# Grouped-query attention of the second mixer: probabilities divided before the value product, values held by TensorE on halves of its columns, result with channels on partitions

## The chip, the cores and the metric

The kernel runs on one core of one Trainium2 chip. The metric is device microseconds (us) of one execution. The kernel before takes 1529.04 us, the median of three runs (1528.59 to 1533.04).

## The reference, cut to what matters

The network is one step of a diffusion model on 256 latent tokens and 256 context tokens of width 1024, with two layers. The first layer has one kind of mixer and a dense feed-forward part; the second has the mixer of this case and a mixture of eight experts. In the second layer only the latent tokens are still needed behind the mixer.

```python
def odd_mixer(h, hc, ...):                         # second layer, need_ctx is False
    q, k, v, gate, xr = split(h @ w_in)            # 8 query heads, 2 key/value heads, 64 each
    qc, kc, vc, gatec, xrc = split(hc @ w_in)
    q = axial_rope(rms_norm(q, qn_g)); k = axial_rope(rms_norm(k, kn_g)); kc = rms_norm(kc, kn_g)
    k_all, v_all = concat([kc, k]), concat([vc, v])        # 512 keys
    s = einsum('bqngd,bknd->bngqk', q, k_all) * 64 ** -0.5
    p = softmax(s, axis=-1)                                # n: 2 key/value heads, g: 4 query heads of each
    y_attn = einsum('bngqk,bknd->bqngd', p, v_all)         # 256 tokens x 512 channels (n, g, d)
    a, bterm = lru_coeffs(conv(xr), ...)                   # for both directions
    y_rec = (linear_scan(forward) + linear_scan(backward)) * gelu(gate)   # 256 x 512
    return concat([y_attn, y_rec])

x = x + g1 * (y @ w_out[1])                        # output projection, 1024 x 1024
x = x + g2 * moe_swiglu(rms_norm(x) * (1 + sc2) + sh2)     # router, top 2 of 8 experts
```

## The kernel before

**Staging.** The program goes through the first layer, then the second mixer, its output projection, the router and the experts. Weights come from HBM through the SyncE queue into a ring of buffers; each dense weight is split on arrival into a rounded part `whi` (ACT, L215) and a remainder `wlo` (DVE L217, during the projection a quarter of it on POOL L219), and a dense product is three TensorE products (L233 to L235). The expert weights are not split; their loads need the numbers of the experts that are used, which the router writes, so they wait in the SyncE queue for DVE's `slot` (L1348).

**What sets the order.** Each engine runs its instructions in the order in which the program writes them. Side work is written as generators: `spawn` starts one, `pump` between the products of a running projection lets each one advance, and `yield n` means that it goes on at the n-th pump from there. So `yield 3` leaves three pumps' worth of other work, on every engine, between what stands ahead of it and what stands behind it. Beside the mixer's own projections (`xr`, then `gate`) these generators run: the recurrence's coefficients and its scans (`lru`, DVE L1049, L1056, L1057, with squares on POOL L1034 and the final sums on POOL L1063, L1064), and the attention.

**The attention.** `attention` starts one `attend1` for each of two query blocks `b` of 128 tokens and four groups `g`, two pumps apart. One of them handles the two heads (n = 0, 1) that share `g`:

- the score product `sp` (128 queries on partitions, 512 keys), one for each head, on 64 rows of TensorE (L1073);
- the softmax: maximum on DVE (L693), exponential on ACT with the sum of its row accumulated into one column of `S` (L694). `P` is not divided;
- `yield 3`, then four 128x128 transposes of `P` for each head into `pt` (L1082), and a copy `PT` to SBUF, by ACT for n = 0 (L1087), by DVE for n = 1 (L1085);
- `yield 1`, then four products for each head (L1093): TensorE holds `PT` (128 keys by 128 queries) and `v` moves, 64 columns, into 64 columns of `po`. `po` has the queries on partitions.

Behind g = 3 come one reciprocal of the eight sums (L1095) and one product of `po` with it into `yr[b]` (L1097): the division of the softmax. There is one `po` for each query block.

**The output projection.** `out_proj` (L643) needs `y` with channels on partitions, in eight tiles of 128 channels, as a rounded part `y1h` and a remainder `y1l`. Tiles 4 to 7 are the recurrence's and already lie so; they are multiplied first. Tiles 0 to 3 are the attention's: `y_tile` transposes two 128x128 blocks of `yr[0]` and `yr[1]` (L1871) and splits the result out of PSUM (L635, L636). A tile is made two tiles ahead of its use. This is done once, for the first 512 output columns; the second 512 use the same tiles. `w_out` of this layer comes as four loads of 512x512 (two halves `h` of the rows, two of the columns), the rows of a load as four blocks of 128 on partitions (`plan_out`, L638).

After the projection come the norm, the router, the gathering of tokens and the experts, which store the result.

## Time and profile before

| What | Value |
|---|---|
| Median of three runs | 1529.04 us (1528.59 to 1533.04) |
| The profiled execution, its own time | 1531.24 us |
| Its span | 1529.4 us |
| TensorE clock granted, mean | 0.984 of full speed |
| PE matmul busy | 1453.7 us, 95% |
| PE weight load busy (overlaps PE) | 866.3 us, 57% |
| DVE busy | 682.0 us, 45% |
| ACT busy | 356.2 us, 23% |
| POOL busy | 145.3 us, 9% |
| Moved by DMA | 400.94 MB, mean 262 GB/s |

The engines' names are those of the profile: PE is TensorE, DVE VectorE, ACT ScalarE, POOL GpSimd, SP SyncE. A row of work gives its start, its duration, the line and tile, shapes as partitions x elements and, in brackets, idle time of the engine ahead of it and what ended it. The averages over the span hide the stages: PE is busy 95% of it, and the share says little of what sets the time in a given stage. The span and the profiled execution's own time differ by 1.8 us, which lies around the span.

### The profile page before, as it was taken

Reading aid. Unit: us, or ns where it says so; the run is one execution under the profiler, and the core shown is the slowest. Engines: PE = TensorE matmul, PEld = TensorE weight load, DVE = VectorE, ACT = ScalarE, POOL = GpSimd, SP = SyncE. Lnnn points to the kernel's source line nnn. Section 1 sums busy time; section 2 is a strip of 40 time slices with the busy share of each in tenths; the row PEclk is TensorE's granted clock in tenths of the full one; section 3 lists DMA queues with packets and bytes.
Section 4 is the critical chain, followed back from the end, with each engine's and each line's share of the span. In section 5 each row is a group of like instructions: output and inputs, shape, how many; then the busy total and the mean of one; then the engine's idle time right before and its main releaser. Section 6 shows DMA issues by size and latency. Waiting matters only on the chain.

```text
span 1529.4 us, 24172 instructions
## 1 busy us (share of the span) xinstructions
PE 1453.7 (95%) x10208; PEld 866.3 (57%) x10208; DVE 682.0 (45%) x1131; ACT 356.2 (23%) x576; POOL 145.3 (9%) x154
## 2 busy tenths in 40 slices
PE   5999899999999999988987999999999999999996
PEld 3766667878788887866666433343433333345442
DVE  3646875787878886387875401010010100011133
ACT  3425442422222222253753100100000000000000
POOL 1230212000000005033224000000000000000000
PEclk9999999999999999999998899999999999999999
DMA  9433454254556684132045899999999999999996
GB/s 349 151 113 108 151 186 145 83 184 146 165 193 199 222 273 132 56 99 82 29 126 217 303 417 417 417 398 369 418 417 418 417 387 418 415 413 415 376 414 250
DMA packets 151798, 400.94 MB, mean 262 GB/s; under 512 B 10185, under 2 KB 38217, under 8 KB 151681
## 3 DMA queue, kind: packets, MB, share of 16 engines
q1 hardware_dynamic: 150688, 396.69, 68.5%
q8 instruction: 82, 1.34, 0.3%
q10 hardware_dynamic: 576, 1.57, 0.3%
q0 software_dynamic: 416, 1.05, 0.3%
q14 instruction: 36, 0.29, 0.1%
HBM read 397.14 MB, written 2.15 MB: 261 GB/s over the span
## 4 chain that ended last, share of the span: by engine, by line
PE 78%; DVE 10%; POOL 4%; ACT 4%; DMA 2%; issue 2%; SPq 0%; DVEq 0%; ACTq 0%; POOLq 0%
PE ph L1548 25%; PE py L1548 12%; PE ph L235 5%; PE ph L234 5%; PE ph L233 5%; PE py L235 3%; PE py L234 2%; PE ps L233 2%; PE ps L234 2%; PE ps L235 2%; PE py L233 2%; PE ph L1552 1%; DVE wlo L217 1%; POOL hrs L240 1%; PE ptg L1596 1%
## 5 line engine op out<-in xcount | busy, mean ns | idle before, releaser
L1548 PE MATMUL ph<-raw,xt 128*32 128x512 f32 (+1 forms) x3840 | 402.1, 558 | 1.1 <-DMA raw<-in_moe_w_dram 1.1
L1548 PEld LDWEIGHTS ph<-raw,xt 128*32 128x32 f32 x3840 | 142.7, 110 | 234.1 <-issue 225.9
L1548 PE MATMUL py<-raw,gt 128*32 128x512 f32 x1760 | 195.6, 592 | 0.0
L215 ACT ACTIVATE whi<-raw 128x2048 fp32r<-128x2048 f32 x58 | 111.1, 1915 | 195.4 <-issue 61.6
L217 DVE TENSOR_TENSOR wlo<-raw,whi 128x2048 fp32r<-128x2048 f32 (+1 forms) x58 | 133.1, 2295 | 47.6 <-ACT whi L215 47.3
L1582 DVE TENSOR_TENSOR silu<-silu,ph 128x512 f32<-128x512 f32 (+3 forms) x33 | 20.6, 623 | 299.8 <-PE ph L1548 266.1
L235 PE MATMUL ph<-hTh,wlo 128*128 128x512 f32 (+1 forms) x384 | 146.2, 381 | 0.8 <-DVE wlo L217 0.8
L234 PE MATMUL ph<-hTl,whi 128*128 128x512 f32 (+1 forms) x384 | 145.3, 378 | 0.0
L233 PE MATMUL ph<-hTh,whi 128*128 128x512 f32 (+1 forms) x384 | 144.6, 377 | 0.0
L1548 PEld LDWEIGHTS py<-raw,gt 128*32 128x32 f32 x1760 | 70.9, 110 | 118.1 <-issue 108.4
L440 DVE SCALAR_TENSOR_TENSOR macc<-raw,cv,macc 128x512 f32<-128x512 f32 x154 | 111.1, 750 | 2.4 <-DMA raw<-in_w_mod_dram 1.2
L233 PE MATMUL ps<-whi,hTh 128*128 128x512 f32 (+1 forms) x272 | 108.4, 404 | 4.0 <-ACT hTh L165 2.1
L234 PE MATMUL ps<-wlo,hTh 128*128 128x512 f32 (+1 forms) x272 | 105.2, 390 | 0.0
L235 PE MATMUL ps<-whi,hTl 128*128 128x512 f32 (+1 forms) x272 | 104.9, 389 | 0.0
L1602 ACT ACTIVATE gt<-ptg 128x512 f32<-128x512 f32 (+3 forms) x18 | 9.5, 529 | 313.6 <-PE ptg L1596 313.6
L234 PEld LDWEIGHTS ph<-hTl,whi 128*128 128x128 f32 x384 | 72.7, 189 | 15.3
L233 PEld LDWEIGHTS ph<-hTh,whi 128*128 128x128 f32 x384 | 73.0, 190 | 14.6
L235 PEld LDWEIGHTS ph<-hTh,wlo 128*128 128x128 f32 x384 | 72.8, 190 | 14.9 <-DVE wlo L217 1.0
L1704 DVE TENSOR_TENSOR yacc<-yacc,py 128x512 f32<-128x512 f32 (+1 forms) x13 | 8.6, 667 | 143.4 <-PE py L1548 110.8
L234 PE MATMUL py<-wlo,gh 128*128 128x512 f32 x176 | 69.1, 393 | 0.4 <-DVE wlo L217 0.4
L233 PE MATMUL py<-whi,gh 128*128 128x512 f32 x176 | 67.8, 391 | 0.0
L235 PE MATMUL py<-whi,gl 128*128 128x512 f32 x176 | 66.9, 395 | 0.0
(362 smaller groups left out, 1748.6 us busy)
## 6 DMA issues: line engine op xcount, KB each, us to landing
raw<-in_moe_w_dram SPq DMA_DIRECT2D x216, 1024.0 KB, 12.7
raw<-in_w_mod_dram SPq DMA_DIRECT2D x48, 1024.0 KB, 5.2
raw<-in_moe_w_dram SPq DMA_DIRECT2D x64, 768.0 KB, 14.9
raw<-in_ffn_w_dram SPq DMA_DIRECT2D x33, 1024.0 KB, 5.3
raw<-in_e_w_in_dram SPq DMA_DIRECT2D x10, 1024.0 KB, 6.9
raw<-in_w_out_dram SPq DMA_DIRECT2D x8, 1024.0 KB, 6.4
raw<-in_o_w_in_dram SPq DMA_DIRECT2D x7, 1024.0 KB, 5.4
ga<-dram SPq DMA_DIRECT2D x6, 512.0 KB, 5.1
```

The lines of the kernel that those rows point to most:

```text
L215: nc.scalar.activation(hi, raw, AF.Copy)
L217: nc.vector.tensor_tensor(lo[:, :, n:], raw[:, :, n:], hi[:, :, n:], op=ALU.subtract)
L233: mm(o, lh, rh, start=start, stop=False)
L234: mm(o, lh, rl, start=False, stop=False)
L235: mm(o, ll, rh, start=False, stop=stop)
L240: g.tensor_tensor(out, out, self.mhalf[:, 0:out.shape[-1]] if len(out.shape) == 2 else self.mhalf, op=ALU.pow)
L440: v.scalar_tensor_tensor(a, raw[:, k], c, a, op0=ALU.mult, op1=ALU.add)
L1548: mm(out[ss, 0:n], lhs[:, ss], w[r][:, cs], start=first, stop=last, tile_position=(0, s * 32))
L1552: mm(out[s * 32:s * 32 + 32, 0:256], lhs, w[:, s * 256:(s + 1) * 256], start=first, stop=last, tile_position=(0, s * 32))
L1582: v.tensor_tensor(s, s, o, op=ALU.mult)
L1596: nc.tensor.transpose(pt[:, f * m:(f + 1) * m], st[t][q][h][0:m, f * 128:(f + 1) * 128], self.ident[0:m, 0:m])
L1602: nc.scalar.activation(dst, src, AF.Copy)
```

## The change

Four things are changed together.

1. The division moves ahead of the transposes. Each step has its own `S` of two columns; right behind the two exponentials DVE takes the reciprocal, and `P` is multiplied by it, on POOL for n = 0 and on DVE for n = 1. The step then waits four pumps instead of three.
2. The value product is turned. TensorE holds `v` (128 keys by 64 channels) on half of its columns, n = 0 on the first, n = 1 on the second, and `PT` moves, 128 queries. The two heads' products alternate. `po` has channels on partitions (n, d), and 128 columns for each `g`. Behind g = 3, `yr[b]` is a copy of `po`.
3. `y_tile` makes tiles 0 to 3 without transposes: two splits out of `yr[0]` and `yr[1]`, each half as wide.
4. The channels of tile g are now (n, d) for one g and not 128 neighbours of (n, g, d), so the rows of `w_out` that meet them are loaded in that order: two loads of 64 partitions in place of one of 128, for both column halves of h = 0.

```diff
--- before.py
+++ after.py
@@ -639,7 +639,12 @@
         for c in range(2):
             for h in halves:
                 src = self.I["w_out"][l, h * 512:(h + 1) * 512, c * 512:(c + 1) * 512]
-                self.plan_w(("out", l, c, h), src.rearrange("(k p) f -> p k f", p=128), (4, 512))
+                if l == 1 and h == 0:
+
+                    parts = [(n * 64, n * 64 + 64, src[n * 256:(n + 1) * 256].rearrange("(k p) f -> p k f", p=64)) for n in range(2)]
+                else:
+                    parts = src.rearrange("(k p) f -> p k f", p=128)
+                self.plan_w(("out", l, c, h), parts, (4, 512))
 
     def out_proj(self, l, y_tile, yT, blocks, halves, gates, done):
 
@@ -1063,18 +1068,22 @@
             nc.gpsimd.tensor_tensor(h[0], h[0], h[1], op=ALU.add)
             nc.gpsimd.tensor_tensor(yr[2 + t // 2][:, (t % 2) * 256:(t % 2 + 1) * 256], h[0], gate[:, t], op=ALU.mult)
 
-    def attend1(self, b, g, po, S, qT, kT, v, yr):
+    def attend1(self, b, g, po, qT, kT, v, yr):
 
         nc = self.nc
         Ps = []
+        S = self.mp.tile([128, 2], F32, tag="ssum8", name="ssum8", bufs=4)
         for n in range(2):
             ns = slice(n * 64, (n + 1) * 64)
             sp = self.ps("sp")
             nc.tensor.matmul(sp, qT[ns, g, b * 128:(b + 1) * 128], kT[ns], start=True, stop=True)
             P = self.row("P")
-            self.softmax(sp, 512, P, S[:, n * 4 + g:n * 4 + g + 1])
+            self.softmax(sp, 512, P, S[:, n:n + 1])
             Ps.append(P)
-        yield 3
+        nc.vector.reciprocal(S, S)
+        for n, P in enumerate(Ps):
+            (nc.vector if n else nc.gpsimd).tensor_scalar(P, P, S[:, n:n + 1], None, op0=ALU.mult)
+        yield 4
         PTs = []
         for n in range(2):
             pt = self.ps("pt")
@@ -1087,14 +1096,13 @@
                 nc.scalar.activation(PT, pt, AF.Copy)
             PTs.append(PT)
         yield 1
-        for n in range(2):
-            h = (n * 4 + g) * 64
-            for kb in range(4):
-                nc.tensor.matmul(po[:, h:h + 64], PTs[n][:, kb * 128:(kb + 1) * 128], v[:, kb, n * 64:(n + 1) * 64], start=kb == 0, stop=kb == 3)
+        for kb in range(4):
+            for n in range(2):
+                ns = slice(n * 64, (n + 1) * 64)
+                nc.tensor.matmul(po[ns, g * 128:(g + 1) * 128], v[:, kb, ns], PTs[n][:, kb * 128:(kb + 1) * 128], start=kb == 0, stop=kb == 3,
+                                 tile_position=(0, n * 64))
         if g == 3:
-            nc.vector.reciprocal(S, S)
-            v3 = lambda a: a.rearrange("p (h d) -> p h d", d=64)
-            nc.vector.tensor_tensor(v3(yr[b]), v3(po), S.unsqueeze(2).broadcast_to([128, 8, 64]), op=ALU.mult)
+            nc.vector.tensor_copy(yr[b], po)
 
     def plan_in1(self):
         w = self.I["o_w_in"][0]
@@ -1176,9 +1184,8 @@
                     yield 1
                 for b in range(2):
                     po = self.ps("po")
-                    S = self.mp.tile([128, 8], F32, tag="ssum8", name="ssum8", bufs=2)
                     for g in range(4):
-                        self.spawn(self.attend1(b, g, po, S, qT, kT, v, yr))
+                        self.spawn(self.attend1(b, g, po, qT, kT, v, yr))
                         yield 2
 
             def conv(t, ps):
@@ -1866,10 +1873,9 @@
 
                     def y_tile(t):
                         if t < 4:
-                            pt = self.ps()[:, 0:256]
                             for b in range(2):
-                                nc.tensor.transpose(pt[:, b * 128:(b + 1) * 128], yr[b][:, t * 128:(t + 1) * 128], self.ident)
-                            self.split_evac(yT[0][:, t], yT[1][:, t], pt)
+                                bs = slice(b * 128, (b + 1) * 128)
+                                self.split(yT[0][:, t, bs], yT[1][:, t, bs], yr[b][:, t * 128:(t + 1) * 128])
                         else:
                             self.split(yT[0][:, t], yT[1][:, t], yr[t // 2][:, (t % 2) * 256:(t % 2 + 1) * 256])
 
```

In the following listings a name with a number is one particular buffer; line numbers of the changed kernel are higher by 5 to 9 (L1056, L1057 become L1061, L1062; L1073 L1079; L1082 L1091; the copy of `pt` into `PT` L1085 becomes L1094; L1093 becomes L1102; L1034 L1039; L1063, L1064 become L1068, L1069). In the changed kernel L1085 is the scaling of `P`.

DVE at the end of the attention, before: the last two copies of `PT`, the scans of the recurrence (L1056, L1057), the reciprocal and the product that ends the attention.

```order
L1085 COPY PT<-pt 128x512
L1057 SCALAR_TENSOR_TENSOR iv_5083<-X,hc,iv_5083 128x256
L1056 SCALAR_TENSOR_TENSOR hc<-xd,iv_5082 128x256
L1049 TENSOR_TENSOR iv_5083<-iv_5083,R 128x512
L1057 SCALAR_TENSOR_TENSOR iv_5082<-xd,hc,iv_5082 128x256
L1056 SCALAR_TENSOR_TENSOR hc<-X,iv_5083 128x256
L1085 COPY PT<-pt 128x512
L1057 SCALAR_TENSOR_TENSOR iv_5083<-X,hc,iv_5083 128x256
L1095 RECIPROCAL ssum_5802<-ssum_5802 128x8
L1097 TENSOR_TENSOR yr<-po,ssum_5802 128x512
```

The same place afterwards, from the copy of `PT` of the last but two step on.

```order
L1094 COPY PT<-pt 128x512
L1083 RECIPROCAL ssum_6027<-ssum_6027 128x2
L1061 SCALAR_TENSOR_TENSOR hc<-X,iv_5083 128x256
L1085 TENSOR_SCALAR P<-P,ssum_6027 128x512
L1062 SCALAR_TENSOR_TENSOR iv_5083<-X,hc,iv_5083 128x256
L1061 SCALAR_TENSOR_TENSOR hc<-xd,iv_5082 128x256
L1094 COPY PT<-pt 128x512
L1062 SCALAR_TENSOR_TENSOR iv_5082<-xd,hc,iv_5082 128x256
L1061 SCALAR_TENSOR_TENSOR hc<-X,iv_5083 128x256
L1062 SCALAR_TENSOR_TENSOR iv_5083<-X,hc,iv_5083 128x256
L1094 COPY PT<-pt 128x512
L1105 COPY yr<-po 128x512
```

The division's two instructions stand between the scans; the scan that stood between the last copy and the attention's end stands ahead of the last copy, and the old reciprocal is gone.

PE at the same place, before: scores `sp`, transposes `pt`, value products `po` of the last three steps, then the first product of the output projection (L233).

```order
L1073 MATMUL sp<-kT_5051,qT_5050 128x512 x2
L1093 MATMUL po<-v_5052,PT 128x64 x8
L1082 MATMUL pt<-cst,P 128x128 x8
L1073 MATMUL sp<-kT_5051,qT_5050 128x512 x2
L1093 MATMUL po<-v_5052,PT 128x64 x8
L1082 MATMUL pt<-cst,P 128x128 x16
L1093 MATMUL po<-v_5052,PT 128x64 x16
L233 MATMUL ps<-whi,y1h 128x512
```

And afterwards.

```order
L1079 MATMUL sp<-kT_5051,qT_5050 128x512 x2
L1091 MATMUL pt<-cst,P 128x128 x8
L1102 MATMUL po<-PT,v_5052 64x128
L1079 MATMUL sp<-kT_5051,qT_5050 128x512 x2
L1091 MATMUL pt<-cst,P 128x128 x2
L1102 MATMUL po<-PT,v_5052 64x128 x7
L1091 MATMUL pt<-cst,P 128x128 x14
L1102 MATMUL po<-PT,v_5052 64x128 x16
L1091 MATMUL pt<-cst,P 128x128 x8
L1102 MATMUL po<-PT,v_5052 64x128 x8
L233 MATMUL ps<-whi,y1h 128x512
```

Each step's `po` now stands ahead of the last transposes of the step behind it, and the last 8 transposes stand behind 16 `po` products of earlier steps; before, 16 transposes stood in a row ahead of the last 16 `po` products.

POOL in the second half of the attention and beside the projection's start, before: squares of the recurrence (L1034), its sums (L1063, L1064) and a quarter of a weight's remainder (L219).

```order
L1034 TENSOR_TENSOR a_5761<-xd 128x512
L1063 TENSOR_TENSOR iv_5082<-iv_5082,iv_5083 128x256
L1034 TENSOR_TENSOR a_5798<-X 128x512
L1063 TENSOR_TENSOR iv_5082<-iv_5082,iv_5083 128x256
L1064 TENSOR_TENSOR yr<-iv_5082,gate_5053 128x256 x2
L1034 TENSOR_TENSOR a_5933<-xd 128x512
L219 TENSOR_TENSOR wlo<-raw,whi 128x4x128
L1034 TENSOR_TENSOR a_5978<-X 128x512
L1063 TENSOR_TENSOR iv_5082<-iv_5082,iv_5083 128x256
L1064 TENSOR_TENSOR yr<-iv_5082,gate_5053 128x256
L1063 TENSOR_TENSOR iv_5082<-iv_5082,iv_5083 128x256
L1064 TENSOR_TENSOR yr<-iv_5082,gate_5053 128x256
```

And afterwards, from the sixth scaling on.

```order
L1068 TENSOR_TENSOR iv_5082<-iv_5082,iv_5083 128x256
L1085 TENSOR_SCALAR P<-P,ssum_5889 128x512
L1039 TENSOR_TENSOR a_5946<-xd 128x512
L1069 TENSOR_TENSOR yr<-iv_5082,gate_5053 128x256 x2
L219 TENSOR_TENSOR wlo<-raw,whi 128x4x128
L1039 TENSOR_TENSOR a_5990<-X 128x512
L1085 TENSOR_SCALAR P<-P,ssum_5972 128x512
L1085 TENSOR_SCALAR P<-P,ssum_6027 128x512
L1068 TENSOR_TENSOR iv_5082<-iv_5082,iv_5083 128x256
L1069 TENSOR_TENSOR yr<-iv_5082,gate_5053 128x256
L1068 TENSOR_TENSOR iv_5082<-iv_5082,iv_5083 128x256
L1069 TENSOR_TENSOR yr<-iv_5082,gate_5053 128x256
```

The scalings stand among the recurrence's instructions, the last two of them ahead of the sums of its last two tiles.

On SP's queue the two loads of `w_out` with h = 0 are two of `64x4x512` in place of one of `128x4x512`; all else stands in the same order, except that one of the two halves of the last of them is issued ahead of the loads of the norm's and router's constants and not behind them.

## Rows read from the trace of the kernel before

**Rows 1.** Busy time by stages, columns as the first line names them
```profile
core 0: us, PE busy (x) PEld busy (x) DVE busy (x) ACT busy (x) POOL busy (x), PEclk, DMA share, GB/s
...
745.00:777.00 32.00, 31.24 (x206) 23.88 (x205) 28.86 (x43) 27.36 (x50) 7.28 (x8) 1.00 0.20 67
777.00:794.00 17.00, 11.44 (x82) 9.56 (x82) 15.30 (x23) 9.73 (x19) 6.27 (x5) 0.94 0.32 108
794.00:812.00 18.00, 17.77 (x74) 13.72 (x74) 9.47 (x20) 6.76 (x11) 6.21 (x5) 0.87 0.91 315
...
900.00:1500.00 600.00, 598.93 (x5792) 231.29 (x5788) 58.27 (x90) 37.73 (x67) 0.00 (x0) 1.00 1.01 408
```

**Rows 2.** SyncE's queue: issue of expert loads (start, us); its wait (us, times, longest)
```profile
847.04 50.68 SPq L208 DMA_DIRECT2D raw<-in_moe_w_dram  x22
...
SPq L1478 <- DVE slot L1348: 15.4, 1, 15.4
```

**Rows 3.** PE in order of time: start, us, line, tile, count, idle before
```profile
751.99 2.00 PE L1093 MATMUL po<-v,PT 128*128 128x64 f32 x16
753.79 0.36 PE L233 MATMUL ps<-hTh,whi 128*128 128x256 f32 x1
...
792.53 1.97 PE L1093 MATMUL po<-v,PT 128*128 128x64 f32 x8 [2.61 <-DVE PT L1085]
```

**Rows 4.** DVE in order of time, columns as in rows 3
```profile
736.08 0.69 DVE L1027 SCALAR_TENSOR_TENSOR iv<-iv,xd 128x512 f32<-128x512 f32 x1 [2.94 <-ACT iv L1024]
...
756.37 0.17 DVE L1095 RECIPROCAL ssum<-ssum 128x8 f32<-128x8 f32 x1
756.47 1.10 DVE L632 SCALAR_TENSOR_TENSOR gate<-gelu,gate 128x256 f32<-128x256 f32 x1
...
758.68 1.52 DVE L1056 TENSOR_TENSOR_SCAN hc<-xd,iv 128x256 f32<-128x256 f32 x1
...
770.36 0.69 DVE L1027 SCALAR_TENSOR_TENSOR iv<-iv,xd 128x512 f32<-128x512 f32 x1 [1.56 <-ACT iv L1024]
...
791.24 0.66 DVE L1056 TENSOR_TENSOR_SCAN hc<-X,iv 128x256 f32<-128x256 f32 x1
791.82 0.66 DVE L1085 COPY PT<-pt 128x512 f32<-128x512 f32 x1
...
794.54 0.69 DVE L1097 TENSOR_TENSOR yr<-po,ssum 128x512 f32<-128x512 f32 x1 [1.31 <-PE po L1093]
```

**Rows 5.** DVE by line and shape: count, busy us, mean ns, idle before
```profile
L713 DVE TENSOR_SCALAR P<-P,ssum,nlam 128x512 f32<-128x512 f32 x8 | 4.4, 545 | 0.3
```

**Rows 6.** POOL: one instruction in time, and one line by shape
```profile
758.12 1.54 POOL L1034 TENSOR_TENSOR a<-X 128x512 f32<-128x512 f32 x1
...
L1760 POOL COPY G2q<-ga 32x256 f32<-32x256 f32 x4 | 1.6, 393 | 0.1
```

**Rows 7.** PE column groups and whole array; then the chain that ended last
```profile
162.20 1.92 PE L388 MATMUL pmod<-raw,cv 128*32 128x512 f32 x16
...
762.08 1.88 PE L1023 MATMUL plru<-xd,bd 128*128 128x512 f32 x4
...
937.71 1.86 PE ph L1548 x16
...
945.04 20.74 PE ph L1548 x192
```

**Rows 8.** PE in the output projection, in order of time
```profile
799.55 0.38 PE L1871 MATMUL ps<-cst,yr 128*128 128x128 f32 x2
...
800.00 0.40 PE L234 MATMUL ps<-wlo,y1h 128*128 128x512 f32 x1
800.24 0.39 PE L235 MATMUL ps<-whi,y1l 128*128 128x512 f32 x1
```

**Rows 9.** SyncE's queue: issue of the last `w_out` load
```profile
799.15 0.71 SPq L208 DMA_DIRECT2D raw<-in_w_out_dram  x1
```

**Rows 10.** DMA issues by line: count, KB each, median us to landing
```profile
raw<-in_w_out_dram SPq DMA_DIRECT2D x8, 1024.0 KB, 6.4
```

## The prediction

> **What bounds the kernel now.** I read the stages first, then the queue that feeds the end, then the chain of waits backwards from there, and last the one engine that the chain names.
>
> The stages [rows 1] split the program behind 730 us into three. From 900 us to the end the DMA share is 1.01 at 408 GB/s: the experts' weights stream without a break, so this part takes the time that its bytes take. What can move is when it starts. The SyncE queue [rows 2] shows that: 22 expert loads go out together at 847.04, and the wait ahead of them (15.4 us) is for DVE's `slot`, the result of the router. Whatever brings the router later by a microsecond brings the end later by one.
>
> Ahead of the router stands the output projection, ahead of that the attention. The projection's first product runs behind the last `po` product on PE, and that one sat 2.61 us idle for DVE's copy of `PT` [rows 3]. That copy starts at 791.82 [rows 4]. DVE is busy 28.86 us of the 32 from 745 to 777, and 15.30 of the 17 from 777 to 794 [rows 1]; most of its own rest in the second is the 1.31 us ahead of `yr`, behind the copy [rows 4]. PE is as full until 777 (31.24 of 32) but has 5.6 us to spare after it. So in the stretch that ends the attention DVE's queue is the bound, PE second; a microsecond of DVE work put ahead of that copy counts, a microsecond taken from PE there mostly doesn't.
>
> **The change part by part.** All differences are to the median of 1529.04. The profiled run took 1531.24 (span 1529.4), 2.2 above the median; the sum is a difference made inside that execution and is put on the median.
>
> *DVE work added.* Each of the eight (query block, group) steps gets a reciprocal of two sums and a scaling of one 128x512 tile. A reciprocal starts at 756.37 and the next instruction at 756.47: 0.10 us. The same scaling in the first layer lasts 0.545 [rows 5]; neighbours overlap a little (a scan of 0.66 us at 791.24 is followed at 791.82 [rows 4]), so I count 0.50. Eight times 0.60 is 4.8. One old reciprocal goes from ahead of the last copy (0.1). By the order, the last step of the recurrence (a scan, 0.66), which stood behind the last copy, now stands ahead of it. Sum 5.4 us.
>
> *What is free of it.* The first two steps fall where DVE idles 2.94 us in one place (ahead of 736.08 [rows 4]): 1.2 us off, 4.2 left. From 745 to 777 DVE idles 3.14 us [rows 1], 1.56 of it in one wait for ACT [rows 4]. The new work fills such holes only if it isn't itself waiting: at the second block's second group the reciprocal stands directly behind its two maxima, so DVE, with everything behind it, waits there for two exponentials on ACT. Bounds 0 and 3.14; I take 1.5 as filled, since half the idle is that one wait and a new wait stands beside it. 2.7 left. `yr` is a copy now and not a product with the sums: same place, same size (0.69), nothing.
>
> *POOL.* It gets eight scalings of 128x512; no row shows this operation there. Below it is a copy of 32x256 at 0.39 us, above it a two-operand product of 128x512 at 1.54 [rows 6]. I take 0.8, as there is one operand, but twice the columns of the copy. POOL itself is free (7.28 of 32 us), and what is queued behind a scaling that waits for DVE's reciprocal are squares and sums of the recurrence and, at the end, the sums that make `yr` of the second half, needed 4 us into the projection. POOL's work is not free for DVE though: while POOL ran the product at 758.12, DVE's scan took 1.52 instead of 0.66, and the one before 1.10 [rows 4, 6]. That is 0.86 lost in 1.54, 0.55 per microsecond of POOL, for instructions with both operands in SBUF; maxima and copies out of PSUM are about half of what runs here, and I put no loss on them. Six scalings of 0.8 at half of 0.55 are 1.3 us; bounds 0 and 6 x 1.54 x 0.55 = 5.1. Sum 4.0.
>
> *PE.* A `po` block of 16 takes 1.80 us now (751.99 to 753.79 [rows 3]). Afterwards two heads share the columns. Upper bound: no overlap, 1.80. Lower: full overlap, 0.90. The nearest row is the modulation's products on four column groups, 16 of 512 columns in 1.92 us, where the whole array takes 1.88 for 4 of them [rows 7]; so they do overlap, and I take 1.0. On DVE's schedule that gain reaches the end only in the last block, and there it is undone: by the order the transposes of the last group stand behind the third group's `po`, which waits for its own copy, so after DVE's last but one copy PE still has 16 products, 8 transposes, one more DVE copy and the last block. Net 0, bounds -1.0 and +1.5.
>
> The Trainium skill (TensorEngine Tiling (Array Packing), Key Properties) says that a change of the tiling mode drains TensorE, which speaks against the halves. The trace agrees as to size: 16 expert products right after transposes take 1.86 us, in an unbroken run of 192 they take 20.74 / 12 = 1.73 [rows 7], 0.13 per return. Two switches in each of eight blocks would be 2 us of PE, inside the bounds above.
>
> *Output projection.* Eight transposes go, in four pairs. A pair starts at 799.55 and the second product behind it at 800.00; one product without it takes 0.24 [rows 8]: a pair costs 0.21, four 0.84. PE is dense there (17.77 us of the 18 from 794 to 812 [rows 1]), so this counts: -0.84. The evacuations from PSUM become splits from SBUF, eight of half the width on ACT and DVE instead of four; they stand behind `yr` with four tiles of products until the first is used: hidden, and if the cover were gone, half a microsecond for the first pair.
>
> *DMA.* Two loads of `w_out` become two halves each. The first is asked for two tiles ahead of its use. The second half of the other is issued where the whole one is now, at 799.15 [rows 9], for the projection's second half of columns, which PE, dense until 812, reaches some 10 us later. A whole one lands in 6.4 us [rows 10], so both are covered; if a half took double, the second would be 3 us late. One half moves ahead of the loads of `BA` in SyncE's queue; its buffer is released by DVE and ACT no later than theirs, so I put nothing on it.
>
> Sum: 5.4 - 1.2 - 1.5 + 1.3 + 0 - 0.84 = +3.2 us, 1532.2. With the bounds: 4.2 - 3.14 + 0 - 1.0 - 0.84 = -0.8 (1528.3) and 4.2 + 5.1 + 1.5 - 0.84 = +10 (1539).
>
> **Rivals.**
> 1. *PE was the bound.* Then eight blocks fall from 1.80 to 1.0 and the pairs go: -6.4 - 0.84, some 1522. For it: PE's 31.24 of 32 us until 777. Against it: PE's long wait at the end is for DVE [rows 3], and DVE's work grows.
> 2. *The two scalings shut each other out.* Both start on the same reciprocal, one on POOL, one on DVE. If the scaling on DVE, and every two-operand instruction beside POOL's, stands still for as long as POOL runs, six times 0.8 to 1.54 is 4.8 to 9.2 instead of 1.3: +6.7 to +11, 1535.7 to 1540; middle 1538. It decides from 0.25 us more per pair than I counted. For it: the row of 1.52; against it: only about half the instructions there can be hit. The Trainium skill (SBUF — State Buffer, Who interferes with whom) states it as a rule: VectorE in a two-port mode, which such a scaling may use, and GpSimd exclude each other for a whole instruction. The slowed scan agrees with exclusion; no row of before has a VectorE scaling beside GpSimd.
> 3. *It changes nothing at the end*, because what DVE gains in work fits in its idle time (3.14 and the 2.94) and the removed pairs pay for the rest: 1529 to 1530.
>
> **How the numbers follow.** Forecast 0.55, rival 1 0.12, rival 2 0.25, rival 3 0.08. The forecast's own range is 1528.3 to 1536. A difference of 0.3% (4.6 us; 1524.4 to 1533.6) is what a measurement can tell from none. Of the forecast's 0.55 I put 0.12 above 1533.6. Faster 0.12; within 0.43 + 0.08 = 0.51; slower 0.12 + 0.25 = 0.37. The range goes from 1526 (part of the way to rival 1) to 1538 (middle of rival 2).
>
> **What would show it.** The first projection product should start at about 798 instead of 794.3, still behind a DVE copy of `PT`, and the expert loads at about 850. DVE's scalings near 0.5 us and POOL's near 0.8 confirm the sizes; scalings of 1 us or more on DVE are rival 2. A `po` block near 1.0 us confirms the halves; if the attention then ends before 790, rival 1 holds. Wrong altogether I am if the span behind 847 changes length, or if a wait for `w_out` appears.

## The result, and the profile after

The changed kernel takes 1548.03 us (median of four runs, 1545.11 to 1551.15), the kernel before 1531.01 us (four runs, 1528.59 to 1533.04). The ratio is 1.0112, with a 95% interval from 1.0097 to 1.0127: slower by 17 us. I had forecast 1532.2 us, 3.2 more than before, with a range to 1538. The profiled execution took 1546.02 us (span 1544.2), 14.8 more than the one of before.

The stages of the changed kernel, to be held against [rows 1]:

```profile
core 0: us, PE busy (x) PEld busy (x) DVE busy (x) ACT busy (x) POOL busy (x), PEclk, DMA share, GB/s
745.00:777.00 32.00, 25.82 (x142) 15.77 (x142) 27.42 (x41) 20.22 (x37) 9.63 (x7) 0.84 0.21 66
777.00:794.00 17.00, 12.57 (x98) 9.04 (x96) 14.89 (x24) 14.99 (x26) 11.26 (x7) 1.00 0.28 93
794.00:812.00 18.00, 13.53 (x81) 10.45 (x82) 13.35 (x31) 5.45 (x18) 5.43 (x5) 0.81 0.47 125
900.00:1500.00 600.00, 597.47 (x5730) 234.99 (x5726) 56.57 (x87) 36.84 (x65) 0.00 (x0) 1.00 1.02 404
```

From 745 to 777 us PE is busy 25.8 of 32 us where it had 31.2, at a mean granted clock of 0.84 where it had 1.00. DVE is no busier. And the stage that I took for fixed, 900 to 1500, moves 404 GB/s instead of 408.

SyncE's queue, the issue of the 272 expert loads that wait for `slot` (eight more go out ahead of it; start, then time from first to last issue), of before and of the changed kernel:

```profile
847.04 651.90 SPq L208 DMA_DIRECT2D raw<-in_moe_w_dram  x272
```

```profile
857.29 658.52 SPq L208 DMA_DIRECT2D raw<-in_moe_w_dram  x272
```

The first load goes out 10.25 us later, and the 272 of them take 6.6 us longer. So there are two losses. The program in five pieces, read in the same way in every run; the marks are the first score product (`sp`), the first projection product, the first and the last expert load:

| us | before | changed | difference |
|---|---|---|---|
| start to first `sp` | 726.95 | 727.55 | +0.6 |
| `sp` to projection | 67.3 | 77.9 | +10.6 |
| projection to first load | 52.8 | 51.8 | -1.0 |
| first to last load | 651.9 | 658.5 | +6.6 |
| last load to end | 30.5 | 28.4 | -2.1 |

The first piece ends between 724.35 and 729.91 in the runs below, also where no edit touches its work, and why is open; so I compare the pieces, and call the second and third together the way from `sp` to the loads: 120.1 us before, 129.7 now.

Where the 10.6 us go shows on PE in order of time (columns as in [rows 3]):

```profile
745.41 0.28 PE L234 MATMUL ps<-hTl,whi 128*128 128x256 f32 x1
745.53 0.28 PE L235 MATMUL ps<-hTh,wlo 128*128 128x256 f32 x1
749.20 0.69 PE L1102 MATMUL po<-PT,v 128*64 128x128 f32 x2 [3.39 <-ACT PT L1096]
749.82 2.08 PE L1028 MATMUL plru<-xd,bd 128*128 128x512 f32 x2
751.82 1.97 PE L1102 MATMUL po<-PT,v 128*64 128x128 f32 x14
753.72 2.01 PE L1028 MATMUL plru<-xd,bd 128*128 128x512 f32 x2
...
759.59 1.09 PE L1102 MATMUL po<-PT,v 128*64 128x128 f32 x16 [0.35 <-ACT PT L1096]
...
765.67 1.02 PE L1028 MATMUL plru<-xd,bd 128*128 128x512 f32 x2
769.13 0.66 PE L1102 MATMUL po<-PT,v 128*64 128x128 f32 x2 [2.44 <-ACT PT L1096]
769.73 2.07 PE L1028 MATMUL plru<-xd,bd 128*128 128x512 f32 x2
771.73 1.50 PE L1102 MATMUL po<-PT,v 128*64 128x128 f32 x14
...
804.46 1.09 PE L1102 MATMUL po<-PT,v 128*64 128x128 f32 x14 [0.31 <-DVE PT L1094]
805.48 0.51 PE L233 MATMUL ps<-whi,y1h 128*128 128x512 f32 x1
```

PE ends a product at 745.8 and waits 3.39 us for ACT's copy `PT`. Behind the wait it is slow: 14 `po` products take 1.97 us where 16 take 1.09 at 759.59, and two `plru` products 2.0 where four take 1.9 before [rows 7]. The same happens, smaller, at 769. The granted clock falls there, shown with the same stretches of before below it:

```profile
core 0: us, PE busy (x) PEld busy (x) DVE busy (x) ACT busy (x) POOL busy (x), PEclk, DMA share, GB/s
...
745.60:749.20 3.60, 0.21 (x3) 0.00 (x1) 3.60 (x4) 3.57 (x8) 0.00 (x0) 0.93 0.22 16
749.20:755.70 6.50, 6.50 (x22) 2.90 (x22) 5.78 (x11) 3.30 (x5) 1.56 (x1) 0.51 0.40 153
755.70:768.00 12.30, 10.64 (x79) 7.78 (x78) 11.14 (x17) 7.76 (x15) 5.55 (x4) 1.00 0.01 1
```

```profile
745.60:749.20 3.60, 2.84 (x22) 2.40 (x21) 3.60 (x5) 3.57 (x8) 0.00 (x0) 1.00 0.25 57
749.20:755.70 6.50, 6.50 (x41) 4.51 (x40) 6.50 (x12) 6.18 (x13) 0.00 (x0) 1.00 0.35 132
```

PE had been busy 0.21 of 3.6 us, and for the 6.5 us that follow it was granted 0.51 of full speed, the lower of its two levels (1.2 and 2.4 GHz), then full speed again. The wait costs its own 3.4 us and, by my estimate from 6.5 us at half of the clock, about as much again behind it.

ACT in the same stretch shows what the copy stood behind:

```profile
740.06 0.81 ACT L1037 ACTIVATE R<-R,cL 128x512 f32<-128x512 f32 x1
740.76 1.91 ACT L215 ACTIVATE whi<-raw 128x2048 fp32r<-128x2048 f32 x1
742.69 1.28 ACT L1051 ACT_TABLE_LOAD   x1
743.99 1.92 ACT L1051 ACTIVATE R<-R 128x2048 f32<-128x2048 f32 x1
745.92 1.28 ACT L699 ACT_TABLE_LOAD   x1
747.21 0.69 ACT L699 ACTIVATE P<-sp,smax 128x512 f32<-128x512 f32 x1
...
748.55 0.59 ACT L1096 ACTIVATE PT<-pt 128x512 f32<-128x512 f32 x1
```

```profile
740.16 0.58 ACT L1087 ACTIVATE PT<-pt 128x512 f32<-128x512 f32 x1
740.64 1.90 ACT L215 ACTIVATE whi<-raw 128x2048 fp32r<-128x2048 f32 x1
742.56 1.28 ACT L1046 ACT_TABLE_LOAD   x1
```

Before, the copy ran at 740.16, ahead of a weight's rounding, a table load, the recurrence's square root, the table load back and two exponentials. Now it is behind all five, at 748.55, though its transposes were done at 741.2. The pause of four pumps in place of three moved it there.

### The profile page after: what moved, and what is told of

Read it like the earlier page. It is cut to its first block, busy times and chain, and to the rows that moved or that the text cites. A ratio compares the mean times of both kernels' runs of the same rounds, so it can differ in the third digit from the quotient of the medians.

```text
span 1544.2 us, 24183 instructions
## 1 busy us (share of the span) xinstructions
PE 1458.3 (94%) x10200; PEld 866.9 (56%) x10200; DVE 690.4 (45%) x1149; ACT 356.8 (23%) x580; POOL 160.0 (10%) x162
## 4 chain that ended last, share of the span: by engine, by line
PE 79%; DVE 9%; ACT 4%; POOL 4%; DMA 2%; issue 2%; SPq 0%; DVEq 0%; ACTq 0%; POOLq 0%
PE ph L1555 25%; PE py L1555 12%; PE ph L235 5%; PE ph L234 5%; PE ph L233 5%; PE ps L233 3%; PE ps L234 3%; PE py L235 3%; PE ps L235 3%; PE py L234 3%; PE py L233 2%; PE ph L1559 1%; POOL hrs L240 1%; DMA raw<-in_moe_w_dram 1%; PE ptg L1603 1%
## 5 line engine op out<-in xcount | busy, mean ns | idle before, releaser
L1555 PEld LDWEIGHTS ph<-raw,xt 128*32 128x32 f32 x3840 | 149.1, 110 | 232.0 <-issue 215.1
L233 PE MATMUL ph<-hTh,whi 128*128 128x512 f32 (+1 forms) x384 | 145.2, 378 | 0.0
L233 PE MATMUL ps<-whi,hTh 128*128 128x512 f32 (+1 forms) x272 | 108.6, 405 | 4.0 <-ACT hTh L165 2.1
L233 PEld LDWEIGHTS ph<-hTh,whi 128*128 128x128 f32 x384 | 72.8, 190 | 14.4
L233 PE MATMUL py<-whi,gh 128*128 128x512 f32 x176 | 68.6, 395 | 0.0
```

The lines of the kernel that those rows point to most:

```text
L233: mm(o, lh, rh, start=start, stop=False)
L1555: mm(out[ss, 0:n], lhs[:, ss], w[r][:, cs], start=first, stop=last, tile_position=(0, s * 32))
```

## The experiments

In all tables "way" is `sp` to first load, "loads" first to last load, each from the profiled execution; the ratio is to runs of the kernel before on the same chip.

| | way | loads | ratio to before (95%) |
|---|---|---|---|
| before | 120.1 | 651.9 | |
| changed | 129.7 | 658.5 | 1.0112 (1.0097 to 1.0127) |
| e1 changed, pause 3 | 123.0 | 658.6 | 1.0075 (1.0061 to 1.0089) |
| e2 before, pause 4 | 130.7 | 651.6 | 1.0080 (1.0064 to 1.0095) |
| e3 changed, DVE scales | 124.7 | 658.3 | 1.0078 (1.0064 to 1.0092) |
| e4 changed, no division | 125.1 | 658.5 | 1.0081 (1.0068 to 1.0094) |
| e5 before, 64 bytes up | 120.7 | 658.3 | 1.0050 (1.0036 to 1.0064) |
| e6 before, loads split | 120.1 | 651.5 | 1.0000 (0.9990 to 1.0011) |
| e7 changed, old addresses | 129.1 | 651.3 | 1.0052 (1.0037 to 1.0067) |
| e8 before, all at 512 | 120.1 | 651.3 | 1.0004 (0.9994 to 1.0015) |
| e9 before, 128 up | 120.4 | 658.1 | 1.0038 (1.0025 to 1.0050) |
| e10 pause 3, DVE scales | 122.8 | 652.5 | 1.0021 (1.0011 to 1.0030) |
| e11 pause 3, no division | 116.2 | 650.7 | 0.9977 (0.9965 to 0.9989) |
| e12 division at the end | 122.1 | 652.2 | 1.0011 (1.0002 to 1.0021) |
| e13 before, 256 up | 120.8 | 651.6 | 1.0010 (1.0001 to 1.0019) |
| e14 before, other seven moved | 120.5 | 651.9 | 1.0024 (1.0014 to 1.0033) |
| e15 division a pump later | 126.2 | 651.8 | 1.0039 (1.0027 to 1.0051) |
| e16 division at the end, early | 118.7 | 652.5 | 0.9996 (0.9986 to 1.0006) |
| e17 before, only buffers up | 120.4 | 657.8 | 1.0024 (1.0015 to 1.0034) |
| e18 tiles up, buffers at 256 | 120.3 | 651.8 | 1.0013 (1.0004 to 1.0023) |

**The pause and the division (e1 to e4).** Theory 1 is the longer pause, its rival the division.

e1, in `attend1`:

```diff
-        yield 4
+        yield 3
```

> The changed kernel with the pause between scaling and transposes back at three pumps; all else as changed. Theory 1 (the longer pause puts ACT's copy of PT behind the square root of the recurrence and its two table loads; PE, whose po product waits for that copy, sits idle 3.4 us and then runs at the lower clock): the wait of 3.39 us near 749 is gone, the last gate product ends near 775 to 777 (changed: 782.9), the expert loads go out near 849 to 852 (changed: 857.3; before: 847.0) and the time is some 6 to 8 us under the changed kernel's. Rival (the division is what costs: POOL's scalings of 1.6 to 2.4 us and DVE's slowed scans make every later step late): the wait moves to the transposes, the loads stay at 855 or later and the time within 2 us of the changed kernel's.

e2, the same line in the kernel before, the other way:

```diff
-        yield 3
+        yield 4
```

> The kernel before with nothing changed but the pause ahead of the transposes, four pumps instead of three. Theory 1 (ACT's copy behind the square root): a wait of 3 to 3.5 us for ACT's PT appears on PE near 746, with the clock lower behind it; the expert loads at 852 to 855 (before: 847.0), the time 5 to 8 us over the kernel before. Rival (the division costs): loads within 2 us of 847, time within 2 us of the kernel before.

e3, both scalings on DVE:

```diff
-            (nc.vector if n else nc.gpsimd).tensor_scalar(P, P, S[:, n:n + 1], None, op0=ALU.mult)
+            nc.vector.tensor_scalar(P, P, S[:, n:n + 1], None, op0=ALU.mult)
```

> The changed kernel with both scalings of P on DVE and none on POOL. Theory 1 (ACT's copy behind the square root): the wait of about 3.4 us near 749 stays, the loads go out within 2 us of 857.3. Rival in its form that POOL is at fault (slow scalings there, and DVE's scans slowed beside them): scans back at 0.66 to 0.75 us, the wait on PE shrinks, loads at 851 to 854 although DVE has eight scalings of 0.5 us more.

e4, no division:

```diff
-        nc.vector.reciprocal(S, S)
-        for n, P in enumerate(Ps):
-            (nc.vector if n else nc.gpsimd).tensor_scalar(P, P, S[:, n:n + 1], None, op0=ALU.mult)
```

> The changed kernel without the division: reciprocal and both scalings are left out, the pause of four pumps stays. Theory 1 (ACT's copy behind the square root): the wait near 746 to 749 stays at about 3.4 us, loads at 852 to 856; what the loads come earlier than 857.3 is the division's own share. Rival (the division costs): loads at 849 or earlier, time within 3 us of the kernel before.

The wait on PE for ACT's copy, in e2 (the kernel before with nothing but the pause) and e4 (no division at all); then PE at the first `po` of e1, where the pause is three again:

```profile
748.89 3.67 PE L1093 MATMUL po<-v,PT 128*128 128x64 f32 x16 [4.36 <-ACT PT L1087]
```

```profile
750.02 0.69 PE L1099 MATMUL po<-PT,v 128*64 128x128 f32 x2 [4.37 <-ACT PT L1093]
```

```profile
741.50 1.24 PE L1102 MATMUL po<-PT,v 128*64 128x128 f32 x16 [0.32 <-ACT PT L1096]
...
748.63 0.65 PE L1091 MATMUL pt<-cst,P 128*128 128x128 f32 x4 [1.39 <-ACT P L699]
```

One more pump in the kernel before brings a wait of 4.36 us and 10.6 us on the way, more than the whole change with its 9.6; e4 keeps a wait of 4.37 without any division. Back at three pumps the wait is 0.32 and the way 6.8 us shorter. So the pause is a cause by itself, and theory 1 holds: e1 came as it said, e4 too in its loads (852.51) though its wait is longer, and e2 is stronger (10.6 us on the way where 5 to 8 were expected). Of the change's 9.6 us on the way 2.9 stay in e1. The rival holds as a second part: e3 keeps the wait (3.38 us at 751), but was to stay within 2 us of the changed kernel by theory 1, and its way is 5.0 shorter. Without POOL's scalings the division costs nothing at four pumps (e3 124.7, e4 125.1). How slow POOL's scalings are, in the changed kernel between 726 and 806 us (columns as in [rows 5]):

```profile
L1085 POOL TENSOR_SCALAR P<-P,ssum 128x512 f32<-128x512 f32 x8 | 15.1, 1887 | 35.6 <-DVE ssum L1083 35.6
...
L1085 DVE TENSOR_SCALAR P<-P,ssum 128x512 f32<-128x512 f32 x8 | 5.2, 646 | 0.1
...
L1039 POOL TENSOR_TENSOR a<-xd 128x512 f32<-128x512 f32 x4 | 4.4, 1093 | 17.9 <-ACT xd L1036 17.9
```

In the mean 1.89 us for a scaling on POOL, longer than the recurrence's squares of the same size there (1.09 and 1.56 for the two kinds of row), and DVE's own scaling 0.65, where e10, without POOL's, has 0.53. Each scaling on POOL starts beside one on DVE, so how long it takes alone isn't shown. A scan of DVE that runs beside POOL takes up to 1.46 us.

**The loads (e5 to e9, e13, e14, e17, e18).** The four experiments above split the loads' time cleanly: 658.3 to 658.6 in variants of the changed kernel, 651.6 to 651.9 in the kernel before and its variant. Besides the split `w_out` loads, the changed kernel has another allocation: four buffers of 32 bytes for `S` where there were two. Everything that the compiled program puts behind them in SBUF lies 64 bytes higher, among it six of the 13 buffers of the expert stream. Before, these six begin at a multiple of 512 bytes, the other seven 128 past one.

```diff
-                    S = self.mp.tile([128, 8], F32, tag="ssum8", name="ssum8", bufs=2)
+                    S = self.mp.tile([128, 8], F32, tag="ssum8", name="ssum8", bufs=4)
```

That is e5; e9 has `bufs=6`, e13 `bufs=10`.

> The kernel before with four buffers instead of two for the tile of the sums, nothing else. It takes 64 bytes more of each partition, and everything allocated behind it in SBUF lies 64 bytes higher, as in the changed kernel; so do 6 of the 13 buffers into which the experts' weights stream (those that began at a multiple of 512 bytes before). Theory A (the stream's 6.6 us come from where these buffers lie): the 272 expert loads take 658 to 659 us from first to last issue instead of 651.9, the first goes out within 1 us of 847.0, the time is 5 to 7 us over the kernel before. Rivals (the stream is slower for the two added loads, or for what the attention does): 651 to 652.5 us and the same time as before.

e6:

```diff
...
+                parts = src.rearrange("(k p) f -> p k f", p=128)
+                if l == 1 and h == 0:
+                    parts = [(n * 64, n * 64 + 64, parts[n * 64:n * 64 + 64]) for n in range(2)]
...
```

> The kernel before with the two loads of w_out (h = 0) split in two halves of 64 partitions each, in the old order of rows; buffers lie as before. Theory A (addresses): expert loads 651 to 652.5 us, first one within 1 us of 847.0, same time as before. Rival (two more loads ahead shift the rotation of queue and semaphores for all loads behind): 658 to 659 us, 5 to 7 us slower.

e7, in the changed kernel (`p` is the mixer's pool):

```diff
-        S = self.mp.tile([128, 2], F32, tag="ssum8", name="ssum8", bufs=4)
...
+                        S = (self.mp, p)[g % 2].tile([128, 2], F32, tag="ssum8", name="ssum8", bufs=2)
...
```

> The changed kernel with its four small tiles of sums put half into a pool that is closed again before the experts, so that all expert buffers lie as in the kernel before; the work is the same. Theory A (addresses): expert loads 651 to 652.5 us, first one at 856 to 858, time about 1539.5, 6 us under the changed kernel. Rivals: 658 to 659 us and the changed kernel's time.

e8, where the tiles `mhalf` and `Z` are then made in `c0`:

```diff
+        self.c0 = es.enter_context(self.pool("const0"))
+        self.wp = es.enter_context(self.pool("weights"))
         self.cp = es.enter_context(self.pool("const"))
         self.xp = es.enter_context(self.pool("xres"))
-        self.wp = es.enter_context(self.pool("weights"))
...
```

> The kernel before with pools opened in another order and 384 bytes of small constants put in front, so that all 13 buffers of the stream begin at a multiple of 512 bytes instead of 6. Theory A (addresses), scaled from 6.6 us for 6 buffers of 13: the loads take 7 to 8 us less than 651.9, some 644, and the time falls to about 1522 to 1524, unless something else bounds the stream then (PE was busy 598.9 of 600 us in it). Rival (any move does harm, the old addresses were only lucky): 655 us or more.

> The kernel before with six buffers for the tile of the sums: everything behind lies 128 bytes higher instead of 64. The buffers that began at multiples of 512 bytes then begin at 128 past one, like the other seven did all along. Theory A in its sharper form (a start off a multiple of 128 bytes is what costs; 64 past one was the fault): the loads take 651 to 652.5 us, time as before. Rival form (any start off a multiple of 512 costs): 658 to 659 us, 5 to 7 us over the kernel before.

> The kernel before with ten buffers for the tile of the sums: everything behind lies 256 bytes higher, the six expert buffers begin 256 past a multiple of 512. If only multiples of 512 are good: 658 us of loads and 5 to 7 us slower than before. If multiples of 256 do: 651 to 652.5 us and the time of before.

e14 is e8 with 64 bytes more of constants in `c0`:

> The kernel before with pools in another order and 448 bytes of small constants in front: the six expert buffers begin at multiples of 512 as before, the other seven at 64 past one. If the stream slows with the number of buffers off 512 only when all are off: 651 to 652.5 us. If 64 is worse than 128 for these seven: 655 us or more.

e17, and e18, which is e5 with `[128, 48]` in this line:

```diff
                     G = self.mod_wide(gp, 1, 2)
+                    gp.tile([128, 16], F32, tag="pad", name="pad")
```

> The kernel before with 64 unused bytes put right ahead of the pool of four of the stream's buffers: these four, the two behind them and the scratch of the experts' stage move by 64 bytes, everything else stays. If the place of the six buffers makes it: 658 to 658.7 us of loads, 5 to 7 us slower than before. If the tiles ahead of them do: 651 to 652.5 us and the time of before.

> As e5 (everything behind the sums 64 bytes higher), with 192 unused bytes more ahead of the four buffers, so that the six buffers of the stream begin 256 past a multiple of 512 and all tiles ahead of them are off by 64. If the place of the six buffers makes it: 651 to 652.5 us of loads. If the tiles ahead do: 658 to 658.7 us.

The stage from 900 to 1000 us, full stream, columns as in [rows 1], of before, e5, e9, e17, e18 and e8 (e13 has 417 GB/s, too):

```profile
900.00:1000.00 100.00, 100.00 (x948) 35.40 (x944) 4.14 (x6) 8.74 (x15) 0.00 (x0) 1.00 1.03 417
```

```profile
900.00:1000.00 100.00, 100.00 (x945) 35.32 (x940) 4.13 (x6) 8.74 (x15) 0.00 (x0) 1.00 1.03 409
```

```profile
900.00:1000.00 100.00, 100.00 (x944) 35.09 (x940) 4.13 (x6) 8.75 (x15) 0.00 (x0) 1.00 1.03 409
```

```profile
900.00:1000.00 100.00, 100.00 (x948) 35.56 (x940) 4.14 (x6) 8.15 (x14) 0.00 (x0) 1.00 1.03 409
```

```profile
900.00:1000.00 100.00, 100.00 (x944) 35.01 (x940) 4.13 (x6) 8.74 (x15) 0.00 (x0) 1.00 1.02 417
```

```profile
900.00:1000.00 100.00, 100.00 (x944) 35.13 (x940) 4.14 (x6) 8.74 (x15) 0.00 (x0) 1.00 1.02 419
```

In this stage the stream runs at 417 GB/s with the six buffers at multiples of 256 bytes (0 or 256 past 512) and at 409 with them 64 or 128 past one, and the loads take 651 to 652 or 658 us with it, whichever attention runs ahead. e6 clears the split loads. e17 and e18 clear the tiles ahead of the buffers; whether the experts' scratch that lies behind the six and moved with them has a part in it is open. My sharper form (128 is enough) was wrong by e9, and the scaling to all 13 buffers was wrong by e8.

The other seven, through which 150 of the 280 loads go, gain next to nothing at 0 (e8: 419 GB/s, loads 0.6 us shorter) and cost no more at 64 than at 128 past (e14: 417). That doesn't clear them: wherever the loads take 658 us they are off multiples of 256 too, so all 13 are, and no run has the six off and the seven on. Whether it is the six or the number of buffers off that counts is not shown.

Why 2% of the rate is 1% of the loads, and why e8 gains nothing, the chain that ended last tells in part. Here are its three pieces from 1280 on (start, us, what), of before and of e5:

```profile
1280.22 8.46 PE py L1548 x79
1288.68 17.62 DMA raw<-in_moe_w_dram
...
1306.35 4.92 PE ph L1548 x36
```

```profile
1280.94 11.84 PE py L1548 x111
1292.78 18.83 DMA raw<-in_moe_w_dram
...
1311.65 4.92 PE ph L1548 x36
```

Until 1280 the chain is PE's, and e5 is as late there as it was at 907 (0.72 us). At 1311.65 it is 5.3 us late: it loses 4.6 us where PE comes up to its loads. So PE sets the pace of most of this stage, and a slower stream counts where the loads' lead is used up.

The times follow less cleanly than the loads. e17, with 657.8 us of loads, is 3.6 us over before where I had expected 5 to 7, and e14, with 651.9 us, is 4.2 us over where none of the pieces from `sp` on is over 0.5 us longer than in the profile of before; the first piece is, with 729.54 us for 726.95. So the case for the addresses rests on the loads' time more than on the ratios.

The Trainium skill (DMA: Bandwidth & Descriptors, How a descriptor splits into AXI transactions) says that a transfer is cut into pieces of 256 bytes, which must start at multiples of 256, so that one that begins off such a multiple fetches bytes that it doesn't use. Its words are for what is read; here it is the place written to that moved. The six buffers agree (417 GB/s at 0 and 256, 2% less at 64 and 128 in this stage); for the seven, 419 against 417 GB/s is the same direction. A rule of this kind would have spoken against this change, and the prediction does not have it.

**What the division costs (e10, e11, e12, e15, e16).** All with three pumps and the old addresses. e10 is e3, e11 is e4 in this form.

> The changed kernel with the pause back at three pumps, both scalings on DVE, and the expert buffers at their old addresses. If the three causes (ACT's copy behind the square root for the longer pause; POOL's slow scalings that hold up DVE beside them; addresses) are all there is and add up: first expert load at 846 to 849, 651 to 652 us of loads, time 1529 to 1532. If the scaling on DVE costs what its 16 instructions of 0.5 us say beside a DVE that is full: 852 or later, 1535 or more.

> The changed kernel with the pause at three pumps, old addresses, and the division (reciprocal and scalings) left out: the new layout alone. If the layout gains on PE (eight po blocks of 1.1 us for 1.8 to 2.0, no transposes in the projection): first expert load at 842 to 845, time 1524 to 1528. If, as I had forecast, PE's gain doesn't reach the end: 845.5 to 847, time 1529 to 1530.

e12, division at the end:

```diff
+        if g == 3:
+            nc.vector.reciprocal(S, S)
+            dg = [self.row("dg") for _ in range(2)]
+            for j in range(4):
+                nc.scalar.activation(dg[0][:, j * 128:(j + 1) * 128], self.ident, AF.Copy, scale=S[:, j:j + 1])
+            nc.vector.tensor_tensor(dg[1].rearrange("p (j q) -> p j q", j=4), self.ident.unsqueeze(1).broadcast_to([128, 4, 128]),
+                                    S[:, 4:8].unsqueeze(2).broadcast_to([128, 4, 128]), op=ALU.mult)
...
+            bc = self.ps("bc")
+            for n in range(2):
+                nc.tensor.matmul(bc[n * 64:(n + 1) * 64], self.ones[:, 0:64], dg[n], start=True, stop=True, tile_position=(0, n * 64))
+            nc.scalar.activation(dg[0], bc, AF.Copy)
...
-            nc.vector.tensor_copy(yr[b], po)
+            nc.vector.tensor_tensor(yr[b], po, dg[0], op=ALU.mult)
```

> A version meant to beat both: the new layout, pause of three pumps, old addresses, and the division at the end as before. Once per query block the reciprocals of the eight sums are put on diagonals of 128x128 (ACT and DVE), two products of 512 columns with ones held by TensorE spread them over the channels' partitions, ACT copies that out of PSUM, and one product of DVE makes yr. It costs PE some 1 us and DVE 0.8 us for each of two blocks in place of 16 scalings. If the scalings were the cost: first expert load at 843 to 847, time 1526 to 1531. If the chain at the end (diagonal, product, copy, product) stands on the path: 849 or later.

e15, against e10. In e16 the division of e12 moves instead, two pumps earlier in the last group of each query block, and ACT makes both copies of `PT` in the last group of the second. e15's edit:

```diff
+        yield 1
         nc.vector.reciprocal(S, S)
...
-        yield 3
+        yield 2
```

> As e10 (pause of three pumps in all, both scalings on DVE, old addresses), but reciprocal and scalings stand one pump behind the exponentials and two ahead of the transposes. From the first score product to the first expert load e10 takes 122.8 us, the version without division 116.2. If DVE's wait for the exponentials, with the recurrence queued behind it, makes the 6.6 us: 118 to 120 and 1530 or less. If the work itself does (16 scalings of 0.5 us): 122 to 123.5 and 1534 as e10.

> As e12 (division at the end by a broadcast through TensorE), but the reciprocal and the diagonals stand two pumps earlier, ahead of the last scans of the recurrence, and ACT makes both copies of PT in the last group. In e12 PE sat 4.08 us idle for ACT's diagonals, which waited for the reciprocal behind DVE's scans. If that wait is the cost: it shrinks under 1.5 us, the span from the first score product to the first expert load is 117 to 119.5 us (e12: 122.1, before: 120.1), the time 1527 to 1530 and under the kernel before. If the scans take the end over: 120 or more and no gain.

The new layout of the value product alone (e11, which leaves the division out) shortens the way by 3.9 us and the time by 0.23%, so it does gain; the range that I gave to the second reading (845.5 or later) is out. With the division ahead of the transposes the way is longer by 6.6 us on DVE alone (e10) and by 6.8 with POOL (e1). So e10's time (0.21% over before) falls between its two readings: the three causes are not all there is. PE's waits from 724 to 806 us in e10, with one of DVE's (us in all, times, longest):

```profile
PE po L1101 <- DVE PT L1093: 6.7, 4, 2.0
...
PE po L1101 <- ACT PT L1095: 3.6, 5, 1.4
...
DVE ssum L1082 <- ACT P L699: 2.8, 3, 1.0
...
PE pt L1090 <- DVE P L1084: 2.2, 1, 2.2
```

DVE waits 2.8 us for the exponentials and has 16 scalings (7.8 us) more in its queue. In e11 PE waits 5.5 us for DVE's copies, 0.6 for ACT's and 2.0 for the exponentials; so with the division it waits longer in several places, and not for DVE's copies alone. What they have in common DVE's own time shows, from the first `sp` to the first projection product (us):

| | `sp` to projection | DVE busy | DVE idle |
|---|---|---|---|
| before | 67.31 | 57.96 | 9.35 |
| e11, no division | 66.44 | 57.65 | 8.79 |
| e1, division on POOL and DVE | 72.20 | 63.48 | 8.72 |
| e10, division on DVE | 73.25 | 64.42 | 8.83 |
| e15, division a pump later | 75.21 | 65.85 | 9.36 |

With three pumps the stretch grows by about what DVE's busy time grows, and its idle time hardly changes: its wait for the exponentials is there, but others of its waits shrink by as much. That speaks for the work and against the wait, which e15 was to tell apart by its time and doesn't: DVE still waited 2.7 us for the exponentials there, PE 10.0 us for DVE's copies, and the way grew to 126.2, beyond both readings. Why DVE is 1.4 us busier in e15 than in e10 is open.

At four pumps it is otherwise: DVE is idle 16.5 us of that stretch in e4 and 10.6 in e3, and e3's way is not the longer one. There the division goes into idle time that the pause has made.

At the end of the attention the division needs no scalings of `P`, but in e12 (way 122.1) PE sat 4.08 us for diagonals whose reciprocal stood behind DVE's scans; e16 takes that to 0.18 and the way to 118.7, under before. Its time is that of the kernel before (0.9996, 0.9986 to 1.0006): no version here that computes all of it beats the kernel before by what can be measured.

## Why the prediction was wrong

**The pause has no term.** The sum lists the instructions added and the copies' place at the end of the attention only. The pause of four pumps is in the diff and in no sentence of the prediction. It moves ACT's copies, and the first lands behind the square root: 5.7 us of the 10.6 on `sp` to projection go when the pause is three again (e1), and 10.5 come with four in the kernel before (67.3 to 77.8, e2). The step "a microsecond taken from PE there mostly doesn't" was the wrong test for it: PE was as full as DVE until 777 ([rows 1]), so a stall of PE there counts, and about doubles by the clock. That is the failed step.

**The span behind 847.** "This part takes the time that its bytes take" failed too: 6.6 us more for the same bytes, of which the shorter end gives 2.1 back. That this span should change length was the sign that I had named for being wrong altogether. The row that I read for it has PE busy 598.93 of 600 us beside the DMA share of 1.01, and in the runs it is PE that leads for most of it. I costed the split loads (rightly at nothing, e6) and didn't look at the allocation that the new tile changes.

**DVE work and what is free of it.** Sum up to POOL +4.0 us at the projection; at three pumps it is +4.9 (67.3 to 72.2, e1), of which the layout takes 0.9 and the division brings 5.8 (66.4 to 72.2). Direction and size held for the part that I had looked at, and the way's +2.9 is near my +3.2. That it is so near is in part luck, for the terms offset each other. I took 2.7 us as filled into DVE's idle time, and that shrank by 0.6 (9.35 to 8.72, e1). I counted 6.7 us of work with POOL's part, and DVE is 5.5 busier. And single sizes were off: DVE's scaling 0.65 us beside POOL for 0.50, POOL's 1.89 for 0.8, over my upper bound of 1.54. For POOL's load on DVE I had 1.3 us: by an estimate from e10, where eight more scalings of 0.53 make DVE only 0.9 us busier than in e1, it is some 3.3.

**PE.** Halves work as I took them: 16 `po` in 1.09 us (1.0). That the gain reaches the end hardly at all in the attention held (0.9 of 5.7 us saved in eight blocks); from the projection to the loads it was 3.0 us in e11 for my 0.84, 1.0 in the changed kernel. Rival 1 is refuted as stated: even without the division 116.2 for 120.1 is 3.9 of its 7.2 us.

**Rival 2** (mutual exclusion) gave the right direction and part of a reason: scans of up to 1.46 and scalings on DVE of up to 0.85 us are there, but POOL against DVE is worth 4.4 to 5.0 us only at four pumps (e7 and the changed kernel against e3) and 0.2 at three (e1 against e10). Its 1538 would have been near e7's 1539.1 for another cause.

## What to carry to other kernels

A pause in pumps is an edit to every queue at once: before costing it, list for each engine what the moved instruction will stand behind, and look above all for table loads and long instructions there. Where PE is near full, as here, a stall of some 3.5 us can cost about double, since the clock fell behind it. And a tile that grows by a few bytes can move the buffers of a stream that is near the bound: compare the addresses of both programs before calling that stage fixed.

## What the runs showed of the hardware that was not expected

- The stream's rate hangs on where its buffers begin: from 900 to 1000 us 419 GB/s with all 13 at multiples of 512 bytes, 417 with seven of them off multiples of 256, 409 with all 13 off. The loads as a whole take 1% longer at 409.
- One tile operand on POOL is no cheaper than two: 1.89 us in the mean for the scaling of 128x512 beside DVE's, 1.09 and 1.56 for the squares.
- 3.6 us of a nearly idle PE (0.21 busy) are followed by 6.5 us at 0.51 of the clock.
- The division by DVE alone costs 6.6 us at three pumps and nothing at four (e10 against e11, e3 against e4): where another wait holds PE already, what hides in it looks free.
